# Placing the mixers' loads further ahead of their use in a woven hybrid trunk

## The chip, the cores and the metric

The kernel runs on one core of one Trainium2 chip. The metric is the device time of one execution in microseconds. Five engines with queues of their own work at once: TensorE (PE; its weight loads are shown as PEld), VectorE (DVE), ScalarE (ACT), GpSimd (POOL) and SyncE (SP), which issues most of the DMAs.

## The reference

One layer of a hybrid trunk over 2048 prompt rows, 16 meta rows and 64 sample rows, 1024 wide, all in float32. Cut to what matters here:

```python
h = rmsnorm(x, norm1_w)
z, xbc, dt, rw_in, hg_in = split(h @ w_in)            # one projection, three groups of heads
y_ssd = group_rmsnorm((ssd_scan(conv(xbc), dt) + d_skip * xs) * silu(z))   # Mamba-2 SSD, 8 heads
y_rw  = (group_layernorm(rwkv7_scan(r, decay, k, v, -kk, kk * a)) + bonus) * g   # RWKV-7, 8 heads
y_hg  = group_rmsnorm(gla_scan(q, k, v, logf)) * silu(gg)                  # HGRN2, 4 heads
x = x + concat(y_ssd, y_rw, y_hg) @ w_out
x = x + (silu(h2 @ w_gate) * (h2 @ w_up)) @ w_down    # h2 = rmsnorm(x, norm2_w)
y = rmsnorm(x, final_norm_w)
```

The scans carry a state from row to row and return their last states. RWKV-7 is

```python
def step(S, inp):                      # per row
    sa = einsum('bhvk,bhk->bhv', S, a)
    S = S * w + sa[..., None] * b + v[..., None] * k
    return S, einsum('bhvk,bhk->bhv', S, r)
```

## The kernel before

Rows are cut into 17 tiles of 128 (the first has 80), tiles into 6 chunks, chunks into 3 blocks. The dense work is a generator: the projection block by block (`projection`), then for three groups of three tiles (`early`) the output projection (`Ffn.out`) and the feed-forward network (`Ffn.ffn`, `Ffn.rest`), the last of them up to its 18th column block. Behind that stand the rest of this network and, for the last eight tiles, another scheme without mixers. Float32 products are made of three fast products of high and low parts; `load_unit` brings a weight and splits it (ScalarE L222, GpSimd or VectorE L224) or, the second time, loads the parts that were kept.

The mixers are generators too. `rw_mixer` does a tile of RWKV-7, `hg_mixer` one of HGRN2 and `ss_mixer` one of SSD. Each loads its rows, which the projection has put into memory (`rin` L541, `hin` L774, `sin`, and `dec` L909), and each ends with a write of its result (`yscr`), from which the output projection reads. `rin`, `hin`, `sin` and `dec` have one buffer each, so a tile's load needs the buffer of the tile before to be free; the last user of `hin` is the write of the HGRN result (L887).

The order of the program is written by a small planner. `flow` runs the dense generator, which yields the cost of each piece (columns divided by 2360, in us), and adds it to `now`. Two streams are stepped whenever their due time has come: RWKV-7 with the costs that `rw_mixer` yields, times `RWX`, and HGRN and SSD together (`hs_mixer`), which take one step each and then wait `HSD`, times `HSX`. So a `yield 8.0` in `rw_mixer` puts 8.0 x 1.08 us of dense work, by the planner's costs, between what stands before and behind it in the program, and an empty `yield` in `hg_mixer` or `ss_mixer` puts 6.0 x 1.03 us there. `drain` steps the streams without dense work until given tiles are done. A scheduler of the framework then makes the queues of the engines from that program, with the program's order as priority.

In `rw_mixer`, 32 x 32 triangular blocks are inverted on VectorE: products (L607) are written to memory (`psc`) and read back in another layout (`Up`, L624), 31 dependent steps of a multiplication and an addition follow (L644, L645), and the result goes through memory again (`psx`: `TT` L655, `XA` L657) before VectorE transposes it (L659) and TensorE uses it.

In `hg_mixer`, step one is the load of `hin`; the next multiplies keys and queries (`key_sums`: product L787 on VectorE, high part L789 on ScalarE, low part L790 on GpSimd), and TensorE sums the parts with a matrix of ones into bank `h`. In `ss_mixer`, step one loads `sin` and `dec` and makes the decays (L911, L912); the next is the product of B and C into bank `h` (with transposes, L919), which VectorE (L922) and ScalarE (L924) empty. There is one bank `h` for both. HGRN's last matmuls of a tile are the transposes of L884.

Between the output projection and the network of a group stands a handoff: VectorE adds the residual (L1201), scales the rows (L250), TensorE transposes them (L256), ScalarE and VectorE split them (L258, L259).

Of the kernel before, what the change touches and what calls it, by code (L numbers as in the profile page):

```python
# [37 lines left out]
GKS = 1  # L38
GLO = 3
URB = 6  # L40
RWX, HSX, HSD = 1.08, 1.03, 6.0
COL = 1 / 2360
AHEAD = 4
KOUT = [8, 9, 10, 11, 0, 1, 2, 3, 4, 5, 6, 7]
# [26 lines left out]
def _bc(ap, dim, n):  # L71
    u = ap.unsqueeze(dim)
    shape = list(u.shape)
    shape[dim] = n
    return u.broadcast_to(shape)


def body(tc, A, O):
# [15 lines left out]
    def mk(p, shape, dt=F32, tag=None, bufs=None):  # L94
        uid[0] += 1
        kw = {} if bufs is None else {"bufs": bufs}
        return p.tile(list(shape), dt, tag=tag, name=f"{tag}_{uid[0]}", **kw)
# [9 lines left out]
    def mm(out, lhsT, rhs, start, stop, more=False):  # L107

        return T.matmul(out, lhsT, rhs, start=start, stop=stop, skip_group_check=more)  # L109
# [119 lines left out]
    def inv_rms(p, ss, n, w, mult, eps):  # L229
        V.tensor_scalar(ss[:n], ss[:n], mult, eps, MUL, ADD)  # L230
        rs = mk(p, [P, w], tag=f"rs{w}", bufs=2)
        G.tensor_tensor(rs[:n], ss[:n], half[:n, 0:w], ALU.pow)  # L232
        return rs
# [301 lines left out]
    def rw_mixer(t):  # L535
# [3 lines left out]
        if t == 0:  # L539
            G.memset(rin[:, :, 80:], 0.0)  # L540
        nc.sync.dma_start(rin[:, :, :n], scr["rw", ci][:, j, :, :n])  # L541
        yield 8.0
        rv, kv, vt = rin[:, 0:4], rin[:, 4:8], rin[:, 8:12]
        S.activation(rin[0:64, 12], rin[0:64, 12], AF.Tanh)
        sg = mk(mx, [P, P], tag="sg", bufs=1)
# [92 lines left out]
            T.transpose(pv[:, p * P:(p + 1) * P], vt[:, p], ident)  # L638
        for cc in range(2):
            S.activation(flat(Z[64:128, cc]), pv[64 * cc:64 * cc + 64, :], AF.Copy)  # L640
        for q in range(31):
            m, w = q // 4 + 1, 31 - q
            tv = by(tp[:, 0:m * w], w)
            V.tensor_tensor(tv, _bc(Xp[:, 0:m, q], 2, w), _bc(Up[:, q, q + 1:32], 1, m), MUL)  # L644
            V.tensor_tensor(Xp[:, 0:m, q + 1:32], Xp[:, 0:m, q + 1:32], tv, ADD)  # L645
            if q % 4 == 3:
                yield 3.5
        yield 1.0
        psx = dram.tile([32, 32, 32], F32, tag="psx", name=f"psx{t}", bufs=2)
        for g in range(4):  # L650
# [4 lines left out]
                nc.sync.dma_start(TT[r, :, 32 * d:32 * d + 32], psx[q0:q0 + 8].rearrange("q i t -> i q t"))  # L655
        XA, XT = ur(), ur()
        nc.sync.dma_start(by(XA[0:32], 32), psx[0:16].rearrange("q i t -> i q t"))  # L657
        yield 6.0
        V.transpose(XT[0:32], XA[0:32])  # L659
        yield 1.0  # L660
        py = cbank()
# [100 lines left out]
    def hg_mixer(t):  # L762
# [10 lines left out]
        else:  # L773
            nc.sync.dma_start(hin, src)  # L774
        Q, F, vi, gate, K = (hin[:, 4 * i:4 * i + 4] for i in range(5))
        yield
        At = mk(mx, [P, 4, P], tag="At", bufs=1)

# [111 lines left out]
    def ss_mixer(t):  # L890
        ci, j = where[t]
        n = LEN[t]
        sin = mk(mx, [P, 12, P], tag="sin", bufs=1)
        src = scr["ss", ci][:, j]
        if t == 0:
            G.memset(sin[:, 0:8, 80:], 0.0)
            nc.sync.dma_start(sin[:, 0:8, :n], src[:, 0:8, :n])
            nc.sync.dma_start(sin[:, 8:12], src[:, 8:12])
        else:
            nc.sync.dma_start(sin, src)  # L900
        x, Bm, Cm, z = sin[:, 0:4], sin[:, 4:6], sin[:, 6:8], sin[:, 8:12]
        ch = chunk[ci]
        dt, cu = ch.dtres[:, 0, j], ch.cu[:, j]
        ex = [ch.ex[:, i, j] for i in range(3)]
        sm = lambda tag, w=8: mk(mx, [P, w], tag=tag, bufs=1)
        tri = triu if t else triu0

        dec = mk(mx, [P, 8, P], tag="dec", bufs=DB)
        nc.sync.dma_start(flat(dec), cscr[ci][j:j + 1].rearrange("o h i -> o (h i)").partition_broadcast(P))  # L909
        for h in range(8):  # L910
            S.activation(dec[:, h, :], dec[:, h, :], AF.Relu, scale=-1.0, bias=cu[:, h:h + 1])  # L911
        S.activation(dec, dec, AF.Exp, scale=-1.0)  # L912
        M2 = [dec[:, 0:4], dec[:, 4:8]]
        yield
        pcb = hbank()
        for g in range(2):
            mm(pcb[:, g * P:(g + 1) * P], Bm[:, g], Cm[:, g], True, True)
        for g in range(2):
            T.transpose(pcb[:, 256 + g * P:256 + (g + 1) * P], Bm[:, g], ident)  # L919
        cB_ = us()  # L920
        cbm = by(cB_[:, 0:256], P)
        V.tensor_tensor(cbm, by(pcb[:, 0:256], P), _bc(tri, 1, 2), MUL)  # L922
        Bt = cB_[:, 256:512]
        S.activation(Bt, pcb[:, 256:512], AF.Copy)  # L924
        for g in range(2):
            V.tensor_tensor(M2[g], M2[g], _bc(cbm[:, g, :], 1, 4), MUL)
        yield

        px = hbank()
        for q in range(4):  # L930
            T.transpose(px[:, q * P:(q + 1) * P], x[:, q], ident)
        xdt = flat(x)
        V.tensor_tensor(h64(xdt), h64(px), _bc(dt, 2, 64), MUL)
        yb = us()
        V.tensor_tensor(h64(yb), h64(px), _bc(cb[:, 16:24], 2, 64), MUL)
        xw = us()
        V.tensor_tensor(h64(xw), h64(xdt), _bc(ex[1], 2, 64), MUL)
        yield
        pY = hbank()
        for h in range(8):  # L940
            for r in (slice(0, 64), slice(64, 128)):
                mm(pY[r, h * 64:(h + 1) * 64], M2[h // 4][:, h % 4, r], xdt[:, h * 64:(h + 1) * 64], True, True)
        V.tensor_tensor(yb, pY, yb, ADD)
        yield
        pI = hbank()
        for g in range(2):
            mm(pI[:, g * 256:(g + 1) * 256], Cm[:, g], Sss[:, g * 256:(g + 1) * 256], True, True)
        yi = flat(M2[0])
        V.tensor_tensor(h64(yi), h64(pI), _bc(ex[0], 2, 64), MUL)
        V.tensor_tensor(yb, yb, yi, ADD)  # L950
        yield
        segs = [(0, P, True)] if t else [(0, 64, True), (64, P, False)]
        for si, (r0, r1, carry_) in enumerate(segs):
            pS = hbank()
            for g in range(2):
                mm(pS[:, g * 256:(g + 1) * 256], Bt[r0:r1, g * P:(g + 1) * P], xw[r0:r1, g * 256:(g + 1) * 256], True, True)
            if carry_:
                V.tensor_tensor(h64(Sss), h64(Sss), _bc(ex[2], 2, 64), MUL)
                V.tensor_tensor(Sss, pS, Sss, ADD)
            else:  # L960
                V.tensor_copy(Sss, pS)
            if t == 0 and si == 0:
                G.dma_start(O["s_ssm"], Sss)
        if t == last_tile:
            G.dma_start(O["p_ssm"], Sss)
        yield
        V.tensor_tensor(yb, flat(z), yb, MUL)
        ss = sm("sss", 2)
        for g in range(2):
            S.activation(yi[:, g * 256:(g + 1) * 256], yb[:, g * 256:(g + 1) * 256], AF.Square, accum_out=ss[:, g:g + 1])  # L970
        rs = inv_rms(mx, ss, P, 2, 1.0 / 256, 4 * EPS)
        for g in range(2):
            S.activation(yb[:, g * 256:(g + 1) * 256], yb[:, g * 256:(g + 1) * 256], AF.Copy, scale=rs[:, g:g + 1])
        yield
        pt = by(hbank(), P)
        for q in range(4):
            T.transpose(pt[:, q, :], yb[:, q * P:(q + 1) * P], ident)
        ys = M2[1]
        V.tensor_tensor(ys, pt, b4(c("ssdw")), MUL)
        G.dma_start(yscr[0][t], ys)  # L980
        done.add((0, t))

    def hs_mixer(t):
        live = [hg_mixer(t), ss_mixer(t)]
        while live:
            live = [g for g in live if next(g, g) is not g]
            yield HSD
# [459 lines left out]
    xs2 = [[dram.tile([P, D], F32, tag=f"xs{h}{j}", name=f"xs{h}{j}") for j in range(NH)] for h in range(2)]  # L1447

    streams += [Stream(mixers("rw", rw_mixer), RWX), Stream(mixers("hs", hs_mixer), HSX)]
    flow(projection())  # L1450
    stG.close()
# [368 lines left out]
```

## Time and profile before

| | us |
|---|---|
| median of 3 runs | 3504.34 (3500.65 to 3512.05) |
| the profiled execution | 3504.96 |
| its span, first to last instruction | 3503.2 |
| TensorE busy | 3364.0 |
| VectorE busy | 2212.7 |
| ScalarE busy | 1227.6 |
| GpSimd busy | 786.6 |
| mean granted TensorE clock | 0.986 of full speed |

The mixers run from 149 us (first load of `rin`) to about 2590 us. "Busy" is the time in which an engine had an instruction in work; the ends of matmuls are modelled, so a busy TensorE is not TensorE at its peak. In a row of waits, the engine named first sat idle until the one behind the arrow was done. In a window row the columns are start and end, length, and the busy time of PE, PEld, DVE, ACT and POOL with the count of instructions, then the granted clock, the DMA engines' busy share and GB/s.

### The profile page before, as it was taken

What the parts mean: (1) busy time and instruction counts of PE and PEld (TensorE: products, weight loads), DVE (VectorE), ACT (ScalarE), POOL (GpSimd) and SP (SyncE); (2) the same over time, 40 slices, a digit from 0 to 9 for tenths busy, and PEclk for the clock granted to TensorE, in tenths of its full rate; (3) what the DMA queues carried; (4) which work ended last, traced back from release to release, by engine and by line L of the source; (5) the groups of instructions that cost most, each with busy time, mean ns of one, the idle gap of its engine ahead of it and who ended that gap; (6) DMA issues with size and microseconds to landing.
All of it is one profiled execution on the core that took longest, in us unless ns stands there. A gap on an engine that the chain in (4) does not pass through costs nothing.

```text
span 3503.2 us, 61013 instructions
## 1 busy us (share of the span) xinstructions
PE 3364.0 (96%) x22588; PEld 2937.2 (84%) x22588; DVE 2212.7 (63%) x4961; ACT 1227.6 (35%) x2635; POOL 786.6 (22%) x1122
## 2 busy tenths in 40 slices
PE   7999999999999999898899999999999999999998
PEld 7999789899789997687777888978888887888787
DVE  3258565477675677777877677676643675665453
ACT  4445333344343343443443222232110352233342
POOL 3324201102112112444442111011100123431101
PEclk9999999999999999899999999999999999999999
DMA  8776875564775667898889997786687568874866
GB/s 315 230 232 212 296 235 163 168 183 161 227 233 181 205 189 271 285 313 302 312 285 356 313 317 268 244 285 197 213 260 260 200 206 272 301 271 164 295 192 215
DMA packets 427124, 860.42 MB, mean 246 GB/s; under 512 B 112433, under 2 KB 212281, under 8 KB 424777
## 3 DMA queue, kind: packets, MB, share of 16 engines
q1 hardware_dynamic: 394376, 749.01, 65.2%
q0 software_dynamic: 32448, 107.50, 8.4%
q8 instruction: 178, 2.92, 0.3%
q14 instruction: 122, 0.99, 0.1%
HBM read 603.81 MB, written 252.54 MB: 244 GB/s over the span
## 4 chain that ended last, share of the span: by engine, by line
PE 70%; DMA 11%; DVE 10%; issue 4%; ACT 2%; SPq 2%; POOL 1%; POOLq 0%; DVEq 0%; ACTq 0%
PE g L109 48%; PE d L109 11%; PE c L109 5%; PE h L109 4%; DMA w<-w 2%; DMA hin<-hg 1%; DVE Xp L645 1%; DMA raw<-in_w_gate 1%; DVE tp L644 1%; DMA hg<-stage 1%; PE po L109 1%; DMA raw<-in_w_up 1%; POOL w L224 1%; DMA x<-in_x_prompt 0%; DMA b4k<-psc 0%
## 5 line engine op out<-in xcount | busy, mean ns | idle before, releaser
L109 PE MATMUL g<-hhi,w 128*128 128x384 f32 (+3 forms) x5424 | 1385.0, 332 | 27.4 <-DMA w<-w 11.4
L109 PEld LDWEIGHTS g<-hhi,w 128*128 128x128 f32 x5424 | 957.9, 189 | 56.2 <-POOL w L224 9.9
L109 PE MATMUL g<-hlo,w 128*128 128x384 f32 (+3 forms) x2736 | 903.1, 330 | 0.0
L109 PEld LDWEIGHTS g<-hlo,w 128*128 128x128 f32 x2736 | 515.4, 188 | 10.0 <-issue 0.9
L224 POOL TENSOR_TENSOR w<-raw,w 128x512 fp32r<-128x512 f32 x180 | 248.7, 1385 | 342.7 <-ACT w L222 313.1
L109 PE MATMUL g<-w,hhi 128*128 128x512 f32 (+1 forms) x832 | 272.4, 406 | 13.8 <-DMA w<-w 6.6
L109 PE MATMUL g<-w,mhi 128*128 128x512 f32 x792 | 264.1, 409 | 10.3 <-DMA w<-w 2.8
L222 ACT ACTIVATE w<-raw 128x512 fp32r<-128x512 f32 x240 | 149.7, 628 | 212.8 <-PE g L109 62.0
L109 PEld LDWEIGHTS g<-w,hhi 128*128 128x128 f32 (+1 forms) x832 | 152.6, 189 | 51.9 <-DMA w<-w 9.9
L109 PEld LDWEIGHTS g<-w,mhi 128*128 128x128 f32 x792 | 147.0, 191 | 47.4 <-DVE acc L1295 3.9
L109 PE MATMUL g<-w,hlo 128*128 128x512 f32 (+1 forms) x416 | 165.5, 399 | 0.0
L644 DVE TENSOR_TENSOR tp<-Xp,b4k 128x60 f32<-128x60 f32 (+24 forms) x527 | 124.5, 236 | 54.5 <-DMA b4k<-psc 41.1
L109 PE MATMUL g<-w,mlo 128*128 128x512 f32 x396 | 158.7, 401 | 0.0
L1295 DVE TENSOR_TENSOR acc<-g,acc 128x512 f32<-128x512 f32 (+1 forms) x198 | 132.6, 681 | 37.3 <-PE g L109 36.9
L109 PE MATMUL g<-w,op 128*128 128x512 f32 x600 | 142.8, 395 | 0.0
L645 DVE TENSOR_TENSOR Xp<-Xp,tp 128x60 f32<-128x60 f32 (+24 forms) x527 | 127.2, 241 | 14.0
L109 PEld LDWEIGHTS g<-w,op 128*128 128x128 f32 x600 | 112.4, 188 | 27.2
L232 POOL TENSOR_TENSOR rs<-ss,half 128x1 f32<-128x1 f32 (+2 forms) x51 | 37.0, 729 | 436.8 <-DVE ss L230 262.1
L360 DVE SCALAR_TENSOR_TENSOR stage<-graw,cvec,stage 128x384 f32<-128x384 f32 (+2 forms) x98 | 53.5, 549 | 115.7 <-ACT graw L355 42.4
L109 PE MATMUL d<-ya,w 128*128 128x512 f32 x528 | 124.4, 392 | 0.0
L109 PEld LDWEIGHTS d<-ya,w 128*128 128x128 f32 x528 | 99.1, 188 | 22.1 <-DMA w<-w 0.5
L109 PE MATMUL d<-w,op 128*128 128x512 f32 x492 | 115.9, 395 | 0.0
(439 smaller groups left out, 5935.5 us busy)
## 6 DMA issues: line engine op xcount, KB each, us to landing
w<-w SPq DMA_DIRECT2D x893, 512.0 KB, 4.3
hin<-hg SPq DMA_DIRECT2D x16, 1280.0 KB, 7.2
rin<-rw SPq DMA_DIRECT2D x16, 896.0 KB, 6.0
raw<-in_w_gate SPq DMA_DIRECT2D x56, 256.0 KB, 4.8
raw<-in_w_up SPq DMA_DIRECT2D x56, 256.0 KB, 4.8
hg<-stage SPq DMA_DIRECT2D x64, 192.0 KB, 2.8
raw<-in_w_out SPq DMA_DIRECT2D x48, 256.0 KB, 4.7
sin<-ss SPq DMA_DIRECT2D x16, 768.0 KB, 5.7
```

What stands on the lines that cost most here:

```text
L109: return T.matmul(out, lhsT, rhs, start=start, stop=stop, skip_group_check=more)
L222: S.activation(hi, raw, AF.Copy)
L224: (G if units[0] % 4 < GLO else V).tensor_tensor(lo, raw, wt[:, 0], SUB)
L232: G.tensor_tensor(rs[:n], ss[:n], half[:n, 0:w], ALU.pow)
L360: V.scalar_tensor_tensor(st[:, a0:a1], raw[:, s0:s0 + a1 - a0], mu, st[:, a0:a1], MUL, ADD)
L644: V.tensor_tensor(tv, _bc(Xp[:, 0:m, q], 2, w), _bc(Up[:, q, q + 1:32], 1, m), MUL)
L645: V.tensor_tensor(Xp[:, 0:m, q + 1:32], Xp[:, 0:m, q + 1:32], tv, ADD)
L1295: V.tensor_tensor(self.acc[:n, i, cs], ps[:n], self.acc[:n, i, cs], ADD)
```

## The change

Only places in the written order are moved. After the load of `rin` 10.0 stands for 8.0; before the 31 steps of the inverse there is a new `yield 3.5`, its groups of four steps yield 3.0 for 3.5, and behind the load of `XA` 7.0 stands for 6.0; HGRN has a second empty step behind its load, and SSD one behind the load of `dec`. `RWX` goes from 1.08 to 1.06 and `HSD` from 6.0 to 5.6.

```diff
-RWX, HSX, HSD = 1.08, 1.03, 6.0
+RWX, HSX, HSD = 1.06, 1.03, 5.6
...
         nc.sync.dma_start(rin[:, :, :n], scr["rw", ci][:, j, :, :n])
-        yield 8.0
+        yield 10.0
...
             S.activation(flat(Z[64:128, cc]), pv[64 * cc:64 * cc + 64, :], AF.Copy)
+        yield 3.5
         for q in range(31):
...
             if q % 4 == 3:
-                yield 3.5
+                yield 3.0
...
         nc.sync.dma_start(by(XA[0:32], 32), psx[0:16].rearrange("q i t -> i q t"))
-        yield 6.0
+        yield 7.0
...
         Q, F, vi, gate, K = (hin[:, 4 * i:4 * i + 4] for i in range(5))
+        yield
         yield
...
         nc.sync.dma_start(flat(dec), cscr[ci][j:j + 1].rearrange("o h i -> o (h i)").partition_broadcast(P))
+        yield
         for h in range(8):
```

## The prediction

> **What bounds the kernel now.** I read the page's first and fourth parts, then the waits of TensorE (the whole run, then two stretches), then short windows for the granted clock, then the order of time around the longest stall.
>
> ```profile
> span 3503.2 us, 61013 instructions
> ...
> PE 3364.0 (96%) x22588; PEld 2937.2 (84%) x22588; DVE 2212.7 (63%) x4961; ACT 1227.6 (35%) x2635; POOL 786.6 (22%) x1122
> ...
> PE 70%; DMA 11%; DVE 10%; issue 4%; ACT 2%; SPq 2%; POOL 1%; POOLq 0%; DVEq 0%; ACTq 0%
> ```
>
> TensorE is busy in 96% of the span and 70% of the last chain runs through it. The change removes no instruction, so it can win only what TensorE idles (3503 - 3364 = 139 us) and what it works at a lowered clock. Who makes it wait, over the run:
>
> ```profile
> PE g L109 <- DMA w<-w: 23.0, 19, 2.9
> PE h L109 <- ACT us L924: 15.4, 4, 6.5
> ...
> PE c L109 <- DVE ur L659: 5.2, 4, 2.0
> ...
> PE h L931 <- DVE At L799: 4.6, 3, 2.2
> ```
>
> The columns are total us, times, longest. The dense weights (w<-w) are not touched by the change. The two rows on bank h are the front of the HGRN and SSD mixers, 20.0 us together, and the row on L659 is the end of the inverse. Where the front's 20.0 us lie (stretch 1400 to 1500, then 1500 to 1900; the fourth stall of L924 is in the order of time below):
>
> ```profile
> PE g L256 <- DVE w2k L250: 4.2, 1, 4.2
> PE h L109 <- ACT us L924: 4.2, 1, 4.2
> ...
> PE h L931 <- DVE At L799: 1.3, 1, 1.3
> ...
> PE h L109 <- ACT us L924: 4.7, 2, 3.1
> ...
> PE h L931 <- DVE At L799: 3.3, 2, 2.2
> ```
>
> The longest one in order of time (start, us, engine; idle before it in brackets):
>
> ```profile
> 2355.40 0.61 PE L109 MATMUL h<-sin 128*128 128x128 f32 x4
> ...
> 2355.90 0.32 SPq L774 DMA_DIRECT2D hin<-hg  x1
> ...
> 2361.96 0.69 DVE L787 TENSOR_TENSOR At<-hin 128x512 f32<-128x512 f32 x1 [1.89 <-DMA hin<-hg]
> ...
> 2362.69 0.63 ACT L789 ACTIVATE us<-At 128x512 fp32r<-128x512 f32 x1 [1.93 <-DVE At L787]
> ...
> 2363.81 1.26 POOL L790 TENSOR_TENSOR us<-At,us 128x512 fp32r<-128x512 f32 x1
> ...
> 2366.41 0.41 DVE L922 TENSOR_TENSOR us<-h,triu 128x256 f32<-128x256 f32 x1
> ...
> 2366.85 0.38 ACT L924 ACTIVATE us<-h 128x256 f32<-128x256 f32 x1 [3.05 <-DVE us L922]
> ...
> 2367.29 1.22 PE L109 MATMUL h<-us,onesr 128*128 128x512 f32 x2 [6.51 <-ACT us L924]
> ```
>
> SSD's B·C product is on TensorE at 2355.4, in the single bank h. VectorE should empty it (L922) but stands at L787, which waits for HGRN's load, issued at 2355.9 and usable at 2362. Behind L787 follows other work, L922 runs at 2366.4, ScalarE's copy L924 at 2366.9, and only then is bank h free for HGRN's first key sums. TensorE lost 6.51 us. The load cannot be issued sooner, because its buffer is freed by the write of the tile before, as the chain in order of time shows for the next tile:
>
> ```profile
> 2479.99 4.48 DMA y<-hin
> 2484.55 6.99 DMA hin<-hg
> ```
>
> The stalls also lower the clock. Windows (PE busy second, then PEld, DVE, ACT, POOL; granted clock, DMA share, GB/s):
>
> ```profile
> 1440.00:1470.00 30.00, 18.63 (x201) 15.82 (x202) 24.57 (x52) 10.63 (x25) 9.55 (x10) 0.66 0.63 210
> 1600.00:1620.00 20.00, 14.54 (x108) 10.88 (x107) 17.41 (x29) 5.13 (x11) 8.71 (x7) 0.83 0.86 288
> 1730.00:1750.00 20.00, 13.23 (x58) 11.56 (x59) 19.49 (x49) 5.16 (x10) 8.22 (x6) 0.83 0.86 315
> 2360.00:2380.00 20.00, 12.00 (x164) 9.56 (x163) 17.66 (x41) 6.54 (x14) 4.44 (x5) 0.74 0.56 165
> 1500.00:1900.00 400.00, 367.89 (x2645) 310.46 (x2643) 322.48 (x667) 164.70 (x363) 172.89 (x140) 0.97 0.89 311
> 1900.00:1945.00 45.00, 41.04 (x339) 33.91 (x339) 32.45 (x83) 15.98 (x42) 8.24 (x13) 0.96 0.91 302
> ```
>
> Busy time times the missing clock is work lost: 18.63 x 0.34 = 6.3 us, then 2.5, 2.2 and 3.1, in all 14.1 us behind the stalls of the front. So what the front costs is at most 20.0 + 14.1 = 34 us, 1.0% of the run.
>
> **The change part by part.** No instruction and no DMA is added or taken away; each queue issues the same ones, in an order that may differ.
>
> The one edit with a price is HGRN's second empty step, with SSD's beside it. Steps of that stream lie HSD x HSX apart: 6.0 x 1.03 = 6.18 us of planned dense work before, 5.6 x 1.03 = 5.77 after. From a tile's last matmuls (L884) to the next tile's B·C product there are two steps before, 12.4 us, and three after, 17.3 us; to the first key sums three before, 18.5, and four after, 23.1. What has to fit into the first distance is the write and the load of the rows above, 4.5 + 7.0, and L787's 0.7: 12.2 us, plus waits between them; into the second also ScalarE's 0.6 and GpSimd's 1.3, 14.1. Before, the fit is exact and any delay ends in a stall; after, 4.9 us more are there. The stall of 6.5 leaves 1.6; the others (4.2, 1.3, and 8.0 in the stretch 1500 to 1900) are shorter than 4.9 each and go. What is late next behind them is VectorE itself, 24.57 of 30 us busy in the window at 1440.
>
> Of that I count only part. From 1500 to 1900 the weights come in at 311 GB/s and a DMA share of 0.89; TensorE idles there for weights as well, and time won at the front is likely handed to the next weight. Those 8.0 us and the 2.5 + 2.2 us of clock I take as zero (bounds 0 and 12.7). At 1440 the front holds 4.2 + 1.3 of 9.7 us of stall (the rest is L250's), so with its share of the clock 5.5 + 6.3 x 5.5 / 9.7 = 9.1 us. At 2361 it is 4.9 us and three quarters of 3.1, 7.2 us. Sum: 16.3 us.
>
> The added yield after the load of dec and the longer one after the load of rin (8 to 10) I price at zero. They are meant for these waits, and in the trace a wait of this sort does not follow the written distance:
>
> ```profile
> ACT dec L911 <- DMA dec<-cu: 50.3, 15, 8.3
> ...
> ACT rin L544 <- DMA rin<-rw: 46.6, 16, 7.0
> ...
> DVE tp L644 <- DMA b4k<-psc: 41.1, 14, 9.2
> ...
> DVE At L787 <- DMA hin<-hg: 31.0, 13, 5.3
> ```
>
> ```profile
> L541 SPq DMA_DIRECT2D rin<-rw x17: 319/326/1052, 148.7 to 2404.3; - x17
> L544 ACT ACTIVATE rin<-rin x17: 309/311/313, 153.6 to 2408.9; 64x128 f32<-64x128 f32 x17
> ```
>
> ```profile
> L109 PE MATMUL c<-rin,wa 64*128 64x128 f32 x272 | 27.4, 291 | 0.1
> ```
>
> ```profile
> L109 PE MATMUL h<-hin x1360: 175/196/377, 446.8 to 2587.6; 128*16 128x16 f32 x77, 128*128 128x128 f32 x58, 128*32 128x32 f32 x39, 128*64 128x64 f32 x19
> ...
> L787 DVE TENSOR_TENSOR At<-hin x17: 677/692/693, 276.9 to 2491.6; 128x512 f32<-128x512 f32 x17
> ```
>
> The last rin load is issued at 2404.3 and ScalarE's tanh starts at 2408.9, 4.6 us later and less than the 8.0 x 1.08 = 8.6 us that the yield put between them. Tile 0's product L787 runs at 276.9, its matmul at 446.8. So ScalarE and VectorE take a mixer's step as soon as its input is expected, and only the always loaded TensorE keeps to the distances. A longer distance then leaves the 46.6 and 50.3 us of idle ScalarE (35% busy) as they are, and TensorE's wait for rin is 0.1 us already. Bounds: 0 and the 0.1.
>
> The inverse: the new 3.5 in front, 7 groups of 3.0 for 3.5 and 7 for 6 behind it. From the load of Up to the matmul that needs the transposed block (L659's) it was 2.16 + 26.46 + 1.08 + 6.48 + 1.08 = 37.3 us and becomes 2.12 + 3.71 + 22.26 + 1.06 + 7.42 + 1.06 = 37.6 us, with RWX 1.08 and 1.06. The groups are VectorE's alone and start when psc has landed. TensorE's 5.2 us on L659 change by at most 4 x 0.3; the bounds are +5 and -1.2, and I take 0.
>
> The pace: RWKV's tile has 76 units at 1.06, 80.6 us, for 73 at 1.08, 78.8; HGRN and SSD take 14 steps of 5.77, 80.8, for 13 of 6.18, 80.3. Adding up all yields of the dense work and the streams, the last HGRN tile is due at 1737 us of dense work instead of 1725, and the RWKV stream's last tile at 1692 instead of 1629. The stretch that covers them ends at 1784, so nothing is left to run uncovered: 0. Without that cover the last HGRN tile would cost its chain, 2587.6 - 2484.6 = 103 us by the rows of its load and of the last matmul on hin; the margin of 47 us stands against it.
>
> Sum: 3504.96 (the profiled execution, span 3503.2; 0.6 us over the median of 3504.34) - 16.3 = 3488.7, say 3489.
>
> [...]
>
> **The rivals.**
>
> *The order goes by readiness, so the front stays.* The rows of rin and At say that the written distances are not kept off TensorE, and at 1440 TensorE itself had run out of dense work (4.2 us on L250), so that it took whatever was ready. If the key sums are again put where their input was expected, the added step is swallowed there. Against it: the order of time at 2355 fits the 12.4 us. Time: 3505, from 3496 to 3514.
>
> *Slower: an inverse falls onto the second handoff.* Between the output projection and the FFN of a token group VectorE has a burst (L1201, L250, L259). By the added yields the handoffs are at 994, 1273 and 1581 us of dense work. The inverse ran at 954 to 982 (tile 9), shortly before the first; at 1211 to 1239 and from 1306, clear of the second; and at 1570, on the third. After, tile 12's runs from 1256 to 1283, right over the second. The first handoff shows the price: 30 us in which TensorE did 18.63 x 0.66 = 12.3 us of work, 17.7 lost. The second lost 45 - 41.04 x 0.96 = 5.6 us. If it becomes like the first, 12.1 us are added; with the first and third as they are, that is 3517. It decides once the other two give back less than 1.6 us. Against it: the first and third handoffs lose their inverse.
>
> *The front's whole cost goes,* also from 1500 to 1900: 34.1 us less the 1.6 left, 3472.5.
>
> **How the numbers follow.** The front's stall goes in the main: 0.47, of which 0.07 for the whole cost; 3489, own range 3472 to 3497. Readiness: 0.33, 3505. Second handoff: 0.20, 3517. The range runs from 3472 to 3518 and leaves under 2 in 10 out. A change of 0.3%, 10.5 us, is about what a measurement of this kernel can tell from none. Of the first case 0.05 ends within it, of the slower one 0.02, and the readiness case gives 0.03 to either side: faster 0.45, same 0.34, slower 0.21.
>
> **What would show it.** Right: the waits of TensorE on L924 fall from 15.4 to under 3 us and on L799 from 4.6 to under 2, the windows behind the first and third handoff show a clock over 0.9, and ScalarE's waits on rin and dec stay near 47 and 50 us. Readiness shows as L924 over 10 us again. The slower case shows as a window under 0.75 near the second handoff (1925 us). A fall of ScalarE's waits on rin and dec to half would make the pricing at zero wrong, and a matmul on hin after 2600 us the cover.

## The result and the profile after

The changed kernel takes 3527.17 us (median of 6 runs, 3525.11 to 3533.7), the kernel before 3506.76 beside it (6 runs): ratio 1.0062, 95% interval 1.0048 to 1.0076. It is slower by 0.6%; 3489 was forecast, and the range ended at 3518. Of the variants below, one execution of jit_rwx took 7407.45 us and is left out of its ratio. In the changed kernel L799 to L931 of before are L801 to L934, L659 is L660 and L924 is L927.

First the page of the kernel after: span, busy time, and the chain that ended last by engine.

```profile
span 3524.6 us, 61009 instructions
...
PE 3364.5 (95%) x22588; PEld 2936.6 (83%) x22588; DVE 2211.1 (63%) x4961; ACT 1234.9 (35%) x2640; POOL 777.1 (22%) x1122
...
PE 64%; DMA 12%; DVE 10%; issue 7%; POOL 3%; ACT 2%; SPq 2%; POOLq 0%; DVEq 0%; ACTq 0%
```

TensorE's busy time is that of before (3364.5 for 3364.0), so all of the 21 us is idle time of TensorE: 160.1 for 139.2 us. Its waits, after:

```profile
PE g L109 <- DMA w<-w: 27.6, 19, 2.8
...
PE g L109 <- DVE w L224: 9.7, 9, 3.8
...
PE c L109 <- DVE ur L660: 8.4, 5, 4.5
...
PE g L109 <- ACT stage L372: 7.0, 3, 4.2
...
PE h L934 <- DVE At L801: 5.4, 2, 3.7
PE g L109 <- DVE stage L380: 5.4, 2, 5.1
PE h L109 <- ACT us L927: 4.5, 2, 3.5
```

The same view of before has for three of these:

```profile
PE g L109 <- DVE w L224: 4.3, 6, 1.6
...
PE g L109 <- DVE stage L380: 0.9, 1, 0.9
...
PE g L109 <- ACT stage L372: 0.9, 1, 0.9
```

The wait that the change aims at fell, from 15.4 to 4.5 us. What rose is scattered, for the most part over lines that the change does not touch: the projection's results (L372, L380) by 10.6 us, weights split on VectorE (L224) by 5.4, the weights' DMA by 4.6, the inverse's result (L659, which it does touch) by 3.2.

Where in the run: windows of both kernels, cut where TensorE had done the same dense work (944.2, 994.1, 1223.2, 1273.1, 1530.8, 1580.7 and 1783.7 us of it by the planner's costs). Rows two, four and six are the three output projections with their handoffs; in the last there are no mixers. Before:

```profile
0.00:1388.00 1388.00, 1336.61 (x10158) 1216.66 (x10159) 857.71 (x2212) 562.87 (x1271) 312.08 (x534) 0.99 0.68 217
1388.00:1491.00 103.00, 87.45 (x726) 72.64 (x725) 69.21 (x165) 41.00 (x93) 37.37 (x33) 0.90 0.85 296
1491.00:1877.00 386.00, 355.74 (x2597) 302.57 (x2597) 307.93 (x623) 162.27 (x354) 172.92 (x137) 0.97 0.89 311
1877.00:1961.00 84.00, 78.19 (x583) 65.34 (x582) 59.42 (x162) 23.50 (x63) 15.20 (x23) 0.98 0.92 309
1961.00:2325.00 364.00, 361.97 (x2653) 320.86 (x2652) 255.07 (x614) 93.40 (x220) 59.00 (x75) 1.00 0.85 290
2325.00:2413.00 88.00, 79.72 (x631) 69.11 (x630) 55.80 (x163) 22.79 (x59) 12.63 (x13) 0.94 0.69 213
2413.00:2688.00 275.00, 265.19 (x1744) 238.77 (x1743) 146.93 (x321) 49.65 (x114) 17.81 (x20) 0.99 0.76 240
2688.00:3503.20 815.20, 799.15 (x3509) 651.19 (x3508) 460.65 (x705) 272.16 (x464) 159.55 (x288) 1.00 0.69 235
```

After:

```profile
0.00:1388.00 1388.00, 1325.74 (x10030) 1210.21 (x10031) 828.85 (x2155) 561.21 (x1257) 308.58 (x530) 0.98 0.68 217
1388.00:1478.00 90.00, 82.28 (x577) 69.28 (x576) 72.24 (x161) 45.12 (x101) 36.28 (x32) 0.94 0.89 312
1478.00:1889.00 411.00, 374.40 (x2901) 315.58 (x2900) 329.07 (x691) 164.04 (x364) 172.99 (x146) 0.97 0.86 301
1889.00:1981.50 92.50, 79.38 (x454) 67.09 (x453) 69.19 (x172) 28.08 (x67) 16.66 (x23) 0.93 0.82 291
1981.50:2346.00 364.50, 356.88 (x2665) 315.35 (x2664) 237.88 (x576) 85.73 (x203) 52.76 (x72) 1.00 0.83 284
2346.00:2420.50 74.50, 70.86 (x436) 61.38 (x435) 51.97 (x141) 23.90 (x57) 6.38 (x9) 0.98 0.67 216
2420.50:2707.00 286.50, 275.19 (x2027) 246.26 (x2026) 161.44 (x362) 55.18 (x129) 24.00 (x26) 1.00 0.75 239
2707.00:3524.60 817.60, 799.76 (x3511) 651.42 (x3509) 460.50 (x705) 271.63 (x464) 159.40 (x288) 1.00 0.69 235
```

Length less PE busy is TensorE's idle time. By row it changes by +10.9, -7.8, +6.3, +7.3, +5.6, -4.6, +1.5 and +1.8 us, in all +21. The first and third handoff give 12.4 us back, the second takes 7.3, and the long dense stretches ahead of them and between them, which I had priced at nothing, take 24 (the last row 1.8 more). TensorE also runs 149 and 195 matmuls fewer in the first and third handoff (577 for 726, 436 for 631): part of the mixers' work there has only moved into the stretches behind them, which have 304 and 283 more.

One of the new waits in detail, the 4.2 us on L372 at 1192 to 1196. The chain of work in order of time there, after (start, us, what):

```profile
1187.81 7.47 DMA hg<-stage
...
1195.36 0.39 ACT stage L372
...
1195.80 1.05 PE g L109 x4
```

and from the DMA issues after, with size and median us from issue to landing, beside the issue of one load in order of time:

```profile
hin<-hg SPq DMA_DIRECT2D x16, 1280.0 KB, 7.8
...
hg<-stage SPq DMA_DIRECT2D x64, 192.0 KB, 2.9
```

```profile
1185.66 0.33 SPq L775 DMA_DIRECT2D hin<-hg  x1
```

The projection's result leaves bank g through `stage`, whose buffer is freed by its write to memory. That write took 7.47 us, not the usual 2.9. It was issued 2.2 us behind HGRN's load of 1280 KB, on which VectorE (L789) still waits until 1194.69. ScalarE stood behind the write and TensorE behind ScalarE. No line of the change touches `stage`; the order has put a mixer's load in front of it. That the load is what slowed the write is likely but not shown: no run moves that load alone.

### The profile page after: what moved, and what is told of

The parts are those of the page before. It is cut to its first block, busy times and chain, and to the rows that moved or that the text cites. A ratio compares the mean times of both kernels' runs of the same rounds, so it can differ in the third digit from the quotient of the medians.

```text
span 3524.6 us, 61009 instructions
## 1 busy us (share of the span) xinstructions
PE 3364.5 (95%) x22588; PEld 2936.6 (83%) x22588; DVE 2211.1 (63%) x4961; ACT 1234.9 (35%) x2640; POOL 777.1 (22%) x1122
## 4 chain that ended last, share of the span: by engine, by line
PE 64%; DMA 12%; DVE 10%; issue 7%; POOL 3%; ACT 2%; SPq 2%; POOLq 0%; DVEq 0%; ACTq 0%
PE g L109 46%; PE d L109 7%; PE c L109 5%; PE h L109 3%; DMA w<-w 3%; DMA raw<-in_w_down 1%; DVE tp L645 1%; DVE Xp L646 1%; DMA hin<-hg 1%; PE po L109 1%; DMA hg<-stage 1%; DMA raw<-in_w_gate 1%; POOL w L224 1%; DMA raw<-in_w_up 1%; DMA b4k<-psc 1%
## 5 line engine op out<-in xcount | busy, mean ns | idle before, releaser
L109 PEld LDWEIGHTS g<-hlo,w 128*128 128x128 f32 x2736 | 516.7, 189 | 10.5 <-DVE hlo L259 1.7
L224 POOL TENSOR_TENSOR w<-raw,w 128x512 fp32r<-128x512 f32 x180 | 245.7, 1370 | 340.0 <-ACT w L222 271.9
```

The source lines that it names most:

```text
L224: (G if units[0] % 4 < GLO else V).tensor_tensor(lo, raw, wt[:, 0], SUB)
```

## The experiments

Theories. *Handoff* (A in the expectations): an inverse that VectorE runs in a handoff costs, the slower rival of the prediction. *Empty steps* (B): those of HGRN and SSD cost or save by themselves. *Pace* (P): RWKV's stream runs slower against the dense work, and that costs. *Distance* (D): the longer waits and closer groups cost wherever they stand. *Chance* (C): every other order makes TensorE meet other late inputs. "Due" places below are the planner's, with its yields followed through. All ratios are to the kernel before on the same chip, from 4 to 12 executions of each variant and 14 to 29 of the kernel before; a ratio is taken over all of them and need not be the quotient of two medians.

**The two halves apart.** HGRN's and SSD's empty steps with `HSD` 5.6, RWKV as before:

```diff
-RWX, HSX, HSD = 1.08, 1.03, 6.0
+RWX, HSX, HSD = 1.08, 1.03, 5.6
+        yield      # hg_mixer, behind the load of hin
+        yield      # ss_mixer, behind the load of dec
```

> HGRN's and SSD's empty steps with HSD 5.6, RWKV-7 as before. Theory A (the loss is RWKV-7's: its inverse now lies over the second handoff, 17 us of dense work before it to 12 behind): this half keeps the gain at the front, faster by 8 to 16 us, TensorE's waits on the copy of bank h (L924 before) under 5 us. Theory B (the empty steps themselves lose, because the pair of streams moves 8 to 12 us of dense work back): slower by 10 to 20 us. Theory C (any move of the order redraws where TensorE meets a late load, and the sum is chance): anywhere within 15 us, and the halves do not add up to the whole.

3522.35 us, ratio 1.0021 (1.0005 to 1.0036).

RWKV's yields and `RWX` as in the change, HGRN and SSD as before:

```diff
-RWX, HSX, HSD = 1.08, 1.03, 6.0
+RWX, HSX, HSD = 1.06, 1.03, 6.0
-        yield 8.0
+        yield 10.0
+        yield 3.5
         for q in range(31):
-                yield 3.5
+                yield 3.0
-        yield 6.0
+        yield 7.0
```

> The RWKV-7 edits alone (10, 3.5, 3.0, 7, RWX 1.06), HGRN and SSD as before. Theory A: slower by 18 to 30 us, since the gain at the front is missing and the second handoff has the inverse; over 5 us more idle TensorE between 944 and 1273 us of dense work. Theory B: within 8 us of before. Theory C: within 15 us of before, no matter which way.

3547.53 us, ratio 1.0093 (1.0072 to 1.0115), some 33 us slower and more than any of the three theories gave. At the change's own `RWX` the loss is the RWKV half. The other half, which carried my whole gain, loses a little alone and mends 0.3% beside it.

**Small changes of pace only**, to see what any other order costs:

```diff
-RWX, HSX, HSD = 1.08, 1.03, 6.0
+RWX, HSX, HSD = 1.075, 1.03, 6.0    # jit_rwx
+RWX, HSX, HSD = 1.08, 1.03, 6.1     # jit_hsd
```

> Before with RWX 1.075 for 1.08 and nothing else: every RWKV-7 step comes half a per cent of its distance sooner, with no wait lengthened or shortened on purpose; the inverse stays clear of the second handoff. Theories A and B: within 5 us of before. Theory C: moves by 5 to 15 us, either way.

> Before with HSD 6.1 for 6.0 and nothing else: the HGRN and SSD stream falls back by 20 us of dense work over the run, more than in the changed kernel (12). Theories A: within 5 us of before. Theory B: slower by 5 to 15 us. Theory C: moves by 5 to 15 us, either way.

3518.11 us, 1.0018 (1.0002 to 1.0034), and 3517.06 us, 1.0022 (1.0006 to 1.0039). A change of half a per cent in `RWX`, or of 1.7% in `HSD`, costs a fifth of a per cent, as hs_only does.

**The second handoff cleared.** The whole change, but a short yield behind rin's load in tiles 9 to 12:

```diff
-        yield 10.0
+        yield 5.0 if t in (9, 10, 11, 12) else 10.0
```

> The changed kernel with 5.0 in place of 10.0 behind the load of rin in tiles 9 to 12, so that the inverse of tile 12 lies 38 to 8 us of dense work before the second handoff instead of over it; the first handoff is met as in the changed kernel. Theory A: 8 to 15 us faster than the changed kernel, that is slower than before by 7 to 14 us, and TensorE's idle time between 1223 and 1273 us of dense work falls from 13 to about 6 us. Theories P and D: slower than before by 15 to 25 us as the changed kernel is.

3535.54 us, 1.0078 (1.0052 to 1.0104). By the plan the inverse of tile 12 ends 8 us ahead of the second handoff, but VectorE did not keep to it. The inverse's multiplications inside the stretch of the second output projection (VectorE's busy time and count, then clock, DMA share, GB/s), for before, after, this kernel, and hit_12 below, in that order:

```profile
1877.00:1961.00 84.00, 6.48 (x31) 0.98 0.92 309
```

```profile
1889.00:1981.50 92.50, 6.20 (x29) 0.93 0.82 291
```

```profile
1889.00:1989.00 100.00, 5.60 (x26) 0.90 0.79 277
```

```profile
1858.70:1948.00 89.30, 6.00 (x28) 0.94 0.80 284
```

Before had all 31 in that stretch too, ended some 9 us ahead of the handoff's burst (first L250); in the three others they run into it. So this kernel cleared nothing, and the theory was still open.

**Pace, inverse and loads, each by itself, to about the same lateness** (last RWKV tile due at 1661 to 1669 us of dense work; before 1629, change 1692):

```diff
-RWX, HSX, HSD = 1.08, 1.03, 6.0
+RWX, HSX, HSD = 1.105, 1.03, 6.0   # rw_pace, nothing else
+        yield 3.5                  # rw_inv: ahead of the groups, RWX 1.08,
+                yield 3.0          #         and in the groups for 3.5
+        yield 10.0                 # rw_load: rin's yield for 8.0, RWX 1.037,
+        yield 7.0                  #          and XA's for 6.0
```

> Before with RWX 1.105 for 1.08 and no other edit: by the yields an RWKV-7 tile takes 91.1 us of dense work (before 88.9, the changed kernel 92.5), no load is moved against its use, and the inverse of tile 12 ends 3 us of dense work before the second handoff. Theory P (what loses is the slower pace of the RWKV-7 stream, wherever the yields stand): slower by 12 to 30 us. Theory A (the inverse over the second handoff): within 8 us of before. Theory D (the longer distances themselves): within 8 us of before.

> Before with the new 3.5 in front of the inverse and its groups at 3.0 for 3.5, RWX 1.08: the yields add up to what they were, but each is rounded up to a whole piece of dense work (1.7 to 2.0 us), so that the tile takes 90.7 us. Second handoff clear. Theory P: slower by 8 to 22 us. Theory A: within 8 us. Theory D: slower by 10 to 25 us if the distance before the inverse is the one that loses, else within 8 us.

> Before with 10 behind rin's load and 7 behind XA's, RWX 1.037, the inverse as before: 90.7 us of dense work for a tile, second handoff clear. Theory P: slower by 8 to 22 us, like the run with the inverse's edits. Theory A: within 8 us. Theory D: slower by 10 to 25 us if these two distances lose, else within 8 us.

3523.31 us, 1.0040 (1.0026 to 1.0053); 3525.04 us, 1.0041 (1.0027 to 1.0055); 3526.92 us, 1.0045 (1.0028 to 1.0062). The same cost whichever way the stream is slowed: it looked like pace.

**Faster pace, without and with the edits:**

```diff
-RWX, HSX, HSD = 1.08, 1.03, 6.0
+RWX, HSX, HSD = 1.02, 1.03, 6.0    # fast_pace, nothing else
+RWX, HSX, HSD = 1.01, 1.03, 6.0    # rw_101, with the RWKV half
+RWX, HSX, HSD = 1.01, 1.03, 5.6    # full_101, with the whole change
+RWX, HSX, HSD = 1.00, 1.03, 5.6    # full_100, with the whole change
```

> RWKV's pace quickened alone: RWX 1.02 for 1.08, all yields as in the kernel before. The stream's last tile is due at 1585 us of dense work for 1629. Pace theory: the three variants that put it at 1661 to 1669 cost 0.40 to 0.45%, so 44 us the other way should gain about as much, ratio 0.995 to 0.997, with TensorE's idle under the 139 us of before. Chance theory (any other order meets other late inputs, and the order of before is a good draw): 1.001 to 1.005, idle 145 us or more.

> All RWKV edits of the change (10.0, 3.5, 3.0, 7.0), HGRN and SSD as before, but RWX 1.01 for 1.06, so that the last tile is due at 1663 as in the three slower variants, not at 1692. Pace theory: 1.004, the 0.5% between this and the RWKV edits at 1.06 (1.0093) being pace. Distance theory (the longer distances themselves lose): it stays at 1.008 to 1.010. Chance theory: anywhere from 1.002 to 1.009.

> The whole change with RWX 1.01 for 1.06: last RWKV tile due at 1663 for 1692. Pace theory: a third of the way back or more, 1.001 to 1.004. Distance theory: 1.006 as the change. Chance theory: 1.002 to 1.009, unrelated to the pace.

> The whole change with RWX 1.00: last RWKV tile due at 1544, 85 us sooner than in the kernel before, though every distance is the change's. Pace theory: faster than before, 0.990 to 0.997. Distance theory: 1.006. Chance theory: 1.002 to 1.009.

1.0031 (1.0015 to 1.0047), 1.0060 (1.0038 to 1.0082), 1.0057 (1.0035 to 1.0078), 1.0019 (1.0006 to 1.0031). The pace theory fails on the fast side: fast_pace should have gained and lost 0.3%. Distance as a fixed price falls with full_100, which has every yield of the change and costs 0.2%. It is no pure test of it: at this `RWX` a tile takes 84.0 us of dense work, for 92.5 in the change.

**Both sides further out, and the empty steps priced at another pace:**

```diff
-RWX, HSX, HSD = 1.08, 1.03, 6.0
+RWX, HSX, HSD = 1.15, 1.03, 6.0    # pace_115, nothing else
+RWX, HSX, HSD = 1.00, 1.03, 6.0    # b100, nothing else
+RWX, HSX, HSD = 0.98, 1.03, 5.6    # full_098, with the whole change
+RWX, HSX, HSD = 1.00, 1.03, 5.6    # hs_100, with the empty steps alone
```

> RWKV's pace alone, far slower: RWX 1.15, all yields as in the kernel before; last RWKV tile due at 1719 us of dense work for 1629, later than in the change (1692). Slow-side theory (what the stream falls behind costs about 0.011% a us, whatever makes it slow): 1.006 to 1.010. Distance theory (the change's longer waits and closer groups themselves lose, pace costs at most the 0.4% seen): 1.002 to 1.005. Chance theory: 1.002 to 1.009, no nearer to the one than the other.

> RWKV's pace alone, far faster: RWX 1.00, last RWKV tile due at 1457, 172 us sooner than before. Symmetric pace theory: fell already with RWX 1.02 (1.0031); it would give 0.985. Slow-side theory: nothing is gained on this side, 0.999 to 1.003. Chance theory: 1.002 to 1.005.

> The whole change with RWX 0.98: every distance is the change's, last RWKV tile due at 1474. Slow-side theory: as the change at RWX 1.00 (1.0019) or a little under, 0.999 to 1.003. Distance theory: 1.006. If the front's 16 us that I had counted are there to be had once the RWKV stream isn't late, it is the first variant under 1: 0.996.

> The empty steps of HGRN and SSD with HSD 5.6, RWKV's yields as before at RWX 1.00. Beside the same pace without the empty steps (run together) it prices those steps by themselves once more: my forecast, 16 us less, ratio of the two 0.995; front's stall gone but nothing gained, as in the pairs run so far (+0.2, -0.3, 0.0%): 0.998 to 1.002 of the other.

3552.9 us, 1.0125 (1.0104 to 1.0147); 1.0068 (1.0049 to 1.0086); 1.0051 (1.0029 to 1.0073); 1.0067 (1.0042 to 1.0092). The factor alone costs up to twice what the change does, and it costs on both sides. hs_100 over b100 is 1.000: with hs_only (+0.2%), the change over rw_only (-0.3%) and full_101 over rw_101 (0.0%) the empty steps are worth nothing on average. The RWKV yields have no fixed price either: full_100 (1.0019) differs in the program from hs_100 (1.0067) by them alone, and there they gain half a per cent, each measured beside the kernel before on a chip of its own. Chance missed too where it had named a size: rw_only, pace_115 and b100 lie above its ranges (15 us, 1.009 and 1.005).

**Late end without handoffs hit, and the reverse.** Only rin's yield differs from the kernel before:

```diff
-        yield 8.0
+        yield 8.0 if t < 13 else 22.0                               # late_end
+        yield 14.0 if 4 <= t <= 9 else 8.0 if t <= 12 else 4.0      # hit_12
```

> The kernel before, with the yield behind rin's load at 22 us from tile 13 on: up to the second handoff the RWKV stream is where it was (inverses of tiles 9 and 12 due 40 to 11 and 62 to 32 us ahead of the first and second handoff), its last tile is due at 1692 us of dense work as in the change, and the inverse of tile 15 ends 26 us ahead of the third handoff. Lateness theory (it costs when the stream ends late): 1.006 to 1.009. Handoff theory (an inverse on the first and second handoff is what costs): 0.998 to 1.002. Chance: 1.002 to 1.009.

> The opposite: the yield is 14 us in tiles 4 to 9 and 4 us from tile 13 on. The inverse of tile 9 is due from 5 to 34 us behind the first handoff, that of tile 12 from 17 ahead to 14 behind the second, both nearly as in the change; tile 16's begins 19 us behind the third, and the last tile is due at 1659. Handoff theory: 1.006 to 1.009. Lateness theory: 1.003 to 1.0045, as the other variants due at 1661 to 1669. Chance: 1.002 to 1.009.

late_end 3506.88 us, 0.9998 (0.9985 to 1.0011): a stream that ends as late as the change's costs nothing. hit_12 3512.62 us, 1.0016 (1.0005 to 1.0027), a quarter of the change's loss, though in the trace VectorE begins the inverse in the bursts (L250) of all three handoffs; only 2 or 3 of its 31 multiplications lie inside each. full_100 tests it harder, with 5, 5 and 7 inside for 0, 3 and 5 in the change, and stands at 1.0019. And b100 has none in any of the three, hs_100 4 or 5 in each, at 1.0068 and 1.0067. The handoff theory's price, 12 us for one, is refuted.

What the front's wait does to the time can be read across these kernels. TensorE's wait on the copy out of bank h, in hs_only, jit_hsd, hit_12, full_100 and late_end:

```profile
PE h L109 <- ACT us L926: 3.1, 1, 3.1
```

```profile
PE h L109 <- ACT us L924: 2.2, 1, 2.2
```

```profile
PE h L109 <- ACT us L924: 1.3, 2, 0.8
```

```profile
PE h L109 <- ACT us L927: 1.9, 1, 1.9
```

```profile
PE h L109 <- ACT us L924: 15.3, 5, 6.5
```

Four of these orders are rid of most of it, one by `HSD` 6.1 and one by rin's yield alone, and all four are 0.16 to 0.22% slower. The one that keeps it is the only one as fast as before. Of the others, full_098 has 3.1 us and costs 0.5%, b100, full_101 and rw_101 have 9.9 to 10.5 and cost 0.6 to 0.7%. So the wait is no measure of the time.

## Why the prediction was wrong

**The front's stall: the wait fell, the credit was wrong.** L924's wait went from 15.4 to 4.5 us (I had said under 3), L799's did not fall (4.6 to 5.4, said under 2). That the empty steps took it away isn't shown: they do in hs_only (15.4 to 3.1), but rw_only, without them, is at 6.0 already, and with them full_101 is at 10.2 for the 10.5 of rw_101 and hs_100 at 7.0 for the 9.9 of b100. At the first and third handoff the idle time fell by 7.8 and 4.6 us, and with the clock (0.90 to 0.94 and 0.94 to 0.98) more; I had counted 9.1 and 7.2. So in this kernel those terms were sized well where they stand; hs_only, with the same empty steps, still idles 12.1 us in its first handoff (1386 to 1477), for 7.7 here. The step that failed is to enter them in the sum as time saved: part of the stretch that went there is work put off, as the counts of matmuls show, the idle time came back elsewhere, and the four pairs put the empty steps' net at zero. The clock, said to be over 0.9 behind the first and third handoff, was 0.83 in the one place and 0.91 in the other; the row between them is behind the second:

```profile
1440.00:1470.00 30.00, 22.35 (x147) 19.95 (x147) 26.70 (x57) 14.09 (x30) 12.39 (x13) 0.83 0.87 292
...
1945.00:1965.00 20.00, 16.35 (x74) 14.40 (x75) 18.39 (x46) 5.09 (x12) 5.43 (x9) 0.74 0.64 201
...
2380.00:2400.00 20.00, 16.36 (x96) 14.24 (x95) 15.88 (x46) 9.34 (x21) 4.86 (x7) 0.91 0.74 253
```

**The pace and the inverse, priced at zero: the failed step that sets the sign.** The RWKV half costs 0.9% alone and 0.4% on top of hs_only (1.0062 over 1.0021). My arithmetic of it was wrong at the start: I multiplied yields by `RWX`, but a step is taken only between whole pieces of dense work, 12 x 384 / 2360 = 1.95 us each for three tiles in the projection. There 3.5 x 1.08 = 3.78 and 3.0 x 1.06 = 3.18 both take two pieces, so the closer groups win nothing; over all tiles they won 2.4 us of the 4.2 that I had, while the new yield added 3.9. A tile went from 88.9 to 92.5 us of dense work (I had 78.8 to 80.6), the inverse from load to use from 40.7 to 43.0 (I had 37.3 to 37.6), all by the planner. My second fault was to ask only whether cover was left at the end. It was: the last matmul on hin starts at 2613.6, in the row

```profile
L109 PE MATMUL h<-hin x1360: 176/196/513, 444.9 to 2613.6; 128*16 128x16 f32 x77, 128*128 128x128 f32 x58, 128*32 128x32 f32 x39, 128*64 128x64 f32 x19
```

which is later than the 2600 that I named as the sign of lost cover, without harm to be seen: the two rows behind the third handoff lose 1.5 and 1.8 us. The cost arises ahead of that, as +10.9, +6.3 and +5.6 us of idle in the dense stretches.

**Yields behind rin and dec.** I said that ScalarE's waits stay near 47 and 50 us. After:

```profile
ACT rin L544 <- DMA rin<-rw: 57.8, 15, 10.3
...
ACT dec L914 <- DMA dec<-cu: 31.8, 10, 8.9
```

The one rose and the other fell by over a third, so the written distance seems to be partly honoured for dec and not for rin. That a longer wait behind rin is worth nothing by itself agrees with late_end and hit_12, which set it to 22 and 14 in some of the tiles.

**The inverse's result.** TensorE's wait on it, 5.2 to 8.4 us, lies inside the +5 to -1.2 that I gave, and not at the 0 that I took. VectorE's own wait for the block's way through memory, before and after:

```profile
DVE ur L659 <- DMA ur<-psx: 26.7, 13, 3.9
```

```profile
DVE ur L660 <- DMA ur<-psx: 41.7, 13, 7.6
```

It is longer by 15 us although 7 stands for 6 behind the load.

**The rivals.** The slower one, 3517, named a place that did get worse: the second handoff idles 13.1 us for 5.8, with a window of 0.74 behind it. Its cause was wrong. I had taken the inverses' places from the planner ("on the third", "clear of the second"); the trace of VectorE has the steps of tile 12 (31, and 29 after) inside the second stretch in both kernels, and hit_12 idles 89.3 - 82.45 = 6.9 us there with the inverse begun in the burst. What TensorE waits for there after is

```profile
PE h L934 <- DVE At L801: 3.7, 1, 3.7
PE g L256 <- DVE w2k L250: 3.5, 2, 2.7
```

In the kernel before the first of these rows is missing there, and the second has 2.8 us. L801 empties bank h of HGRN's key sums. In the change it meets the handoff: ahead of it VectorE ran the three residual adds (L1204, L1201 before), 2.1 us, and of the inverse only one multiplication and one addition, 0.4 us. So 3.7 of the 5.4 us of the front's second wait now stand in the second handoff. Readiness is refuted for the front by the sign that I gave (L924 fell below 10) but had the right sum for it: no time saved.

**What is shown and what stays open.** Shown: at the change's `RWX` of 1.06 its loss comes with its RWKV half, and neither the late end of the stream, nor a longer distance behind rin's load, nor an inverse in the handoffs costs that much. Shown as well: of the 18 other orders none is faster and one is equal, and `RWX` alone costs 0.2 to 1.25% away from 1.08, to both sides. If the factors of before had been chosen by timing, an order that is hard to beat would be no surprise; no run here tells. What the order of before does better is seen only as many small waits that it does not have (stage buffers, split weights, the inverse's result). Which of these meetings carries how much of the 0.6% wasn't settled, and so the cause of the loss stays open below the level of the half: none of the runs removes one of them by itself, with another buffer for `stage` for instance.

A granted clock of 0.83 or 0.74 is a mean. In the stretches of 3.41 us below, cut so that its changes (at 1938.2, 1941.6 and 1945.0 us) fall between them, it is 1.00 or 0.50; after, around the two waits on L801 and L250 above:

```profile
1934.78:1938.19 3.41, 0.00 (x0) 0.00 (x0) 3.34 (x15) 1.45 (x4) 0.57 (x1) 1.00 1.02 393
1938.19:1941.60 3.41, 3.31 (x22) 2.90 (x23) 3.41 (x10) 1.11 (x3) 0.33 (x1) 0.50 0.73 291
1941.60:1945.02 3.42, 0.88 (x28) 0.74 (x25) 3.42 (x8) 1.11 (x4) 2.00 (x3) 1.00 0.00 1
1945.02:1948.43 3.41, 2.40 (x10) 2.10 (x10) 3.41 (x11) 1.20 (x2) 0.39 (x2) 0.50 0.32 109
1948.43:1951.84 3.41, 2.07 (x4) 1.17 (x4) 3.02 (x7) 0.63 (x1) 0.94 (x3) 0.50 0.69 206
```

In these rows the clock is at half in the stretch behind one in which TensorE did little (0.00, then 0.88 us of work), even where it is itself busy for 3.31 us, and stays at half behind one with 2.40 us of work. The stretch ahead was not always idle throughout: the one at 1941.60 has 2.54 us of idle, all of it in the one wait of 2.66 us on L250, and the next is at half.

## What to carry to other kernels

A stall removed at one place of a woven schedule is a gain only if the work that filled the stretch isn't put off to another; compare counts of instructions at equal progress before booking it. When a change of written distances moves a whole stream, price the stream's new meetings with every queue and buffer at more than zero, in the stretches where the bound engine is busy over 90% already, and read where an engine really runs its steps from the trace, not from the planner. Before trusting such an edit, time a change of half a per cent in its pace: here that alone cost 0.2%, a third of what the change does. And price an edit in more than one order: the RWKV half cost 0.4% beside the empty steps at `RWX` 1.06, and its yields gained 0.5% at 1.00.

## What the runs showed that I had not expected

An order reproduces its waits: late_end, which differs from before only from tile 13 on, has 15.3 us on L924 for 15.4, and 3365.0 us of busy TensorE for 3364.0. Between orders the busy time of the same 22588 matmuls is not constant: 3362.0 us in full_100, 3391.7 in pace_115. And single executions of one kernel spread as far as the effects looked for (hs_only 3507.5 to 3532.1 us in 12 runs), so the stretches of one profiled execution carry a sign only where several kernels agree.
